# Layer one's attention in stated order on ScalarE and VectorE, without the gates' sum up to the query

## The chip, the cores and the metric

One core of a Trainium2 chip. The metric is the device time of one execution in microseconds; smaller is better. Before the change the median of three runs is 624.39 us (624.07 to 624.49).

## What is computed

Two decoder layers over 256 tokens of width 1024, in float32. Each layer: a norm, one input projection, 12 self-attention heads and 4 heads that attend to 256 memory tokens, an output projection, and a SwiGLU FFN. Layer one's self-attention is the forgetting attention; layer two's has ALiBi slopes instead (with 256 tokens all keys lie in the query's own block).

```
def fox_attention(q, k, v, log_f):
    F = jnp.cumsum(log_f, axis=-1)
...
        s = (jnp.einsum('bhqd,bhkd->bhqk', qb, k).astype(jnp.float32) * scale
             + Fq[..., :, None] - F[..., None, :])
        s = jnp.where(tq[:, None] >= kpos[None, :], s, NEG)
        p = jax.nn.softmax(s, axis=-1)
...
xn = rms_norm(h, norm_mix[i]); mn = rms_norm(mem, norm_mem[i])
...
h = h + heads @ w_out[i]
hn = rms_norm(h, norm_ffn[i])
gu = hn @ w_gate_up[i]
h = h + (jax.nn.silu(gu[..., :D_FF]) * gu[..., D_FF:]) @ w_down[i]
```

`Fq` is the gates' sum up to the query. It is the same number for every key of a query, that is, along a softmax row.

## The kernel before

Every float32 product is made of three matmuls: operands are split into a rounded part (`hi`) and the rest (`lo`), and `prod` (L317) issues hi·hi, lo·hi and hi·lo. Weights stream from HBM in units of up to 1 MB. `split` (L212) halves a unit and splits each half, 128x1024: the rounded part on ScalarE (L224), the rest on VectorE (L227), which needs ScalarE's result. `weights` (L233) calls `split` so that the splits are stated five halves ahead of their use. A unit's buffer is loaded again (L204, on SP's queue) when its last `lo` is made.

`mixer` (L466) is a layer's attention. The value projection comes first. Then three groups `g` of query and key projections (L574 to L601), each for two pairs of heads, 8 steps of 12 matmuls. Before group 1 `memory_heads` (L552) runs: in layer one the memory's key and value projection (`mem_kv`, L340), whose row factors come from two mean squares on ScalarE (`factor`, L257, called at L360) with a power on POOL, then the memory heads' queries (`qm`). After each group the queries and keys are scaled and split (L591 to L601), on ScalarE, VectorE and POOL. Then the output projection (L612), 12 matmuls of 512 columns to a step, and what is left of attention.

Attention itself is a generator for each pair of heads, `attend` (L393). Those alive are advanced by `step()` (L460), once for every two of the 8 projection steps and once for each step of the output projection, so that attention's parts lie between projection matmuls. Its parts, with waiting steps between them: the bias (`bias`, L534) and the score matmuls with bias, maximum, exponentials (L425), reciprocal and products (L429) in one step; two or three steps later the transposes (L436) and their copies out of PSUM (L439 on ScalarE, L440 on VectorE); two steps later the product with the values, and the split of the result into the output projection's operand (L449, by `split_ps`, L245 and L246). In the trace `s_`, `p_`, `pT_` and `o_` are scores, probabilities, their transposes and the outputs; `_m` is memory, `_s` self-attention.

`gate_sums` (L514) makes the sums over the gates: `F_ps` and its copy `fr`, which goes through DRAM to all partitions (`fd`, then `fk`), and `Fq_ps` with its copy `fq`, the sums up to the query. `bias` makes, for a pair of heads in layer one, F minus Fq plus the mask in four VectorE instructions. `wake_exp` (L452) loads the exponential's table early.

PSUM has 8 banks in one pool, `probs` 3 buffers, `work` 7. The whole program runs with TensorE and SP in the order in which it is written (L773). ScalarE, VectorE and POOL are ordered by a planner, by when it believes each instruction ready and by priority, which falls in the order of writing; only layer one's value projection (L479) has ScalarE and VectorE in written order too. Within such a stretch the written order is kept for each engine; where the stretch's instructions fall among those outside it stays the planner's.

Of the kernel before, what the change touches and what calls it, by code (L numbers as in the profile page):

```python
# [27 lines left out]
P = 128  # L29
# [29 lines left out]
TURN_STEPS = 2  # L59

# [78 lines left out]
def trunk(ctx: ExitStack, tc: tile.TileContext, plan, stream, x, gains, norm_final, square, mem, out):  # L139
# [23 lines left out]
    mem_t = [ap.tile([P, 2, 512], F32, tag="probs", name=f"mem{t}", bufs=3).rearrange("p a s -> p (a s)") for t in range(NT)]  # L163
# [176 lines left out]
    def mem_kv(i):  # L340
# [5 lines left out]
        for u in range(2):  # L346
            for kk in range(4):
# [11 lines left out]
                if i == 0 and k == 3:  # L359
                    rs_mem.extend(factor(mem_t[t], f"mem{t}") for t in range(NT))  # L360
# [32 lines left out]
    def attend(name, xq, xk, vt, h0, idle, bias, dst, kt):  # L393
# [16 lines left out]
        pr = ap.tile([P, 2, 512], F32, tag="probs", name=f"p_{name}", bufs=3)  # L410
        for a in range(2):
            for qt in range(NT):
                c = slice(qt * S, qt * S + nk[qt] * P)
                if causal:
                    nc.vector.tensor_tensor_reduce(pr[:, a, c], sb[a].t[:, c], more[qt][:, a], scale=-1.0, scalar=-NEG,  # L415
                                                   op0=ALU.add, op1=ALU.min, accum_out=nmax[:, a, qt:qt + 1])
                else:
                    nc.vector.tensor_reduce(nmax[:, a, qt:qt + 1], sb[a].t[:, c], axis=AX.X, op=ALU.max, negate=True)
        total = sp.tile([P, 2, NT], F32, tag="total", name=f"total_{name}")
        rc = sp.tile([P, 2, NT], F32, tag="rc", name=f"rc_{name}")  # L420
        for a in range(2):
            for qt in range(NT):
                c, j = slice(qt * S, qt * S + nk[qt] * P), slice(qt, qt + 1)
                src, scale = (pr[:, a, c], -1.0) if causal else (sb[a].t[:, c], 1.0)
                nc.scalar.activation(pr[:, a, c], src, AF.Exp, bias=nmax[:, a, j], scale=scale, accum_out=total[:, a, j])  # L425
            nc.vector.reciprocal(rc[:, a], total[:, a])
            for qt in range(NT):
                c = slice(qt * S, qt * S + nk[qt] * P)
                nc.vector.tensor_scalar_mul(pr[:, a, c], pr[:, a, c], rc[:, a, qt:qt + 1])  # L429
        for _ in range(SOFTMAX_STEPS[causal]):  # L430
            yield
# [5 lines left out]
        pT = ap.tile([P, 2, 512], F32, tag="probs", name=f"pT_{name}", bufs=3)  # L437
        width = len(blocks) * P
        nc.scalar.activation(pT[:, 0, :width], tb[0].t[:, :width], AF.Copy)  # L439
        nc.vector.tensor_copy(pT[:, 1, :width], tb[1].t[:, :width])  # L440
# [8 lines left out]
        split_ps(dst[0][:, kt, :], dst[1][:, kt, :], ob.t[:, :S])  # L449
        yield  # L450

    def wake_exp(src):  # L452

        one = sp.tile([P, 1], F32, tag="one", name="one", bufs=1)
        nc.scalar.activation(one, src, AF.Exp, scale=0.0)
# [10 lines left out]
    def mixer(i, xs, rs):  # L466
# [44 lines left out]
        if i == 0:  # L511
            fq = cp.tile([P, NT, H], F32, name="fq")

        def gate_sums():  # L514
# [19 lines left out]
        def bias(h0):  # L534

            b = fk[:, h0:h0 + 2]
            if i == 1:
                return b[:, :, P:], b
            b0 = ap.tile([P, 2, P], F32, tag="bias", name=f"bias{h0}", bufs=1)
            for a in range(2):  # L540
# [33 lines left out]
        for g in range(3):  # L574
            if g == MEM_AT[i]:
                memory_heads()
            kb = [bank(f"qk_ps{i}{2 * g + a}") for a in range(2)]
            for k in range(KD):
                wh, wl = weights(U["qk", i, g][k // 4], k % 4)
                for a in range(2):  # L580
                    for s in range(2):
                        c = slice(a * P, (a + 1) * P)
                        prod(kb[a], kb[a].t[:, s * S:(s + 1) * S], (wh[:, s, c], wl[:, s, c]),
                             (xs[0][:, k, :], xs[1][:, k, :]), k == KD - 1)
                if k % 2:
                    step()
            if g == 0:
                rsb = spread(rs, f"x{i}", (DH ** -0.5, 1.0), "x")
                if i == 0:
                    active.append(gate_sums())  # L590
            for a in range(2):  # L591
                p = 2 * g + a
                qk = ap.tile([P, 2, S], F32, tag="work", name=f"qk{i}{p}", bufs=WORK_BUFS)
                nc.vector.tensor_mul(qk.rearrange("p a s -> p (a s)"), kb[a].t, rsb.rearrange("p a s -> p (a s)"))
                xq = ap.tile([P, 2, S], F32R, tag="work", name=f"xq{i}{p}", bufs=WORK_BUFS)
                xk = ap.tile([P, 2, 2 * S], F32R, tag="pair", name=f"xk{i}{p}", bufs=PAIR_BUFS)
                no_lo(xk)
                split_queries(xq, qk[:, 0])
                split_keys(xk, qk[:, 1])
                idle = a + IDLE[i][g]  # L600
                active.append(attend(f"s{i}{p}", xq, xk, vsb, 2 * p, idle, bias, hT, p))  # L601

        acc = [[bank(f"o_acc{i}{t}{c}") for c in range(2)] for t in range(NT)]

        def o_item(n, j, kk, t, halves=(0, 1)):
            k = 2 * j + kk
            wh, wl = weights(U["out", i][n], kk)
            for c in halves:
                cs = slice(c * 512, (c + 1) * 512)
                prod(acc[t][c], acc[t][c].t, tok(hT, k, t), (wh[:, 0, cs], wl[:, 0, cs]), n == 3 and kk == 1)  # L610

        for n, j in enumerate((3, 0, 1)):  # L612
            for kk in range(2):
                step()
                for t in range(NT):
                    o_item(n, j, kk, t)
        while active:
            step()
# [29 lines left out]
    def ffn(i, xs, late):  # L648
# [5 lines left out]
        def gu(c, kk):  # L654
# [13 lines left out]
            if first:  # L668
                rsb.append(spread(rs, f"f{i}", (1.0,), "f")[:, 0])
# [156 lines left out]
```

## Time and profile before

| | |
|---|---|
| median of three runs | 624.39 us |
| profiled execution | 623.77 us |
| its span, first to last instruction | 622.0 us |
| TensorE, VectorE, ScalarE, POOL busy | 608.5, 455.8, 392.4, 61.6 us |
| layer one's attention and projections | about 11 to 129 us |
| layer one's FFN | 129 to 313 us |
| layer two's attention and projections | 314 to 430 us |
| layer two's FFN and the final norm | 430 to 622 us |

Times in the profile are microseconds from the span's start. A wait is idle time of an engine just before an instruction, with the instruction that ended it. PE is TensorE, DVE is VectorE, ACT is ScalarE, SPq is SP's queue. The profiled execution took 1.77 us more than its span.

### The profile page before, as it was taken

The numbers are of one execution on the slowest core, as the hardware profiler recorded it, in microseconds if no ns is written. First come the engines' busy times: TensorE is split into PE (matmuls) and PEld (weight loads), VectorE is DVE, ScalarE is ACT, GpSimd is POOL, SyncE is SP. The second block draws the span as 40 slices with busy tenths as digits, with TensorE's granted clock in tenths as the row PEclk, the third lists the DMA queues.
The fourth block names the chain that finished last, engine by engine and source line by source line (L and its number), as shares of the span: only waits on it lengthen the run. The fifth ranks groups of instructions, "written<-read, shape, count | busy, mean of one in ns | idle before, by whom it ended". The sixth has DMA issues, their size and how long they took to land.

```text
span 622.0 us, 9564 instructions
## 1 busy us (share of the span) xinstructions
PE 608.5 (98%) x3640; PEld 533.9 (86%) x3640; DVE 455.8 (73%) x827; ACT 392.4 (63%) x737; POOL 61.6 (10%) x90
## 2 busy tenths in 40 slices
PE   8999999999999999999999999999999999999995
PEld 6999887788888888888899999877888888888884
DVE  5677999978677676678675679986867666666664
ACT  7879788575555555557467589865755555555542
POOL 2023122046000000000011032200000000000000
PEclk9999999999999999999999999999999999999999
DMA  8977431525455545555455642332455555555301
GB/s 354 420 276 273 169 136 69 202 96 214 174 195 204 193 173 184 194 203 190 165 187 203 243 144 89 136 135 99 155 191 199 204 188 173 184 199 203 136 1 67
DMA packets 16774, 112.31 MB, mean 181 GB/s; under 512 B 1996, under 2 KB 2008, under 8 KB 4312
## 3 DMA queue, kind: packets, MB, share of 16 engines
q1 hardware_dynamic: 16440, 111.42, 49.1%
q8 instruction: 28, 0.46, 0.3%
q10 hardware_dynamic: 288, 0.29, 0.1%
q14 instruction: 18, 0.15, 0.1%
HBM read 110.64 MB, written 1.06 MB: 180 GB/s over the span
## 4 chain that ended last, share of the span: by engine, by line
PE 81%; DVE 9%; ACT 7%; issue 1%; DMA 1%; SPq 0%; POOLq 0%; POOL 0%; DVEq 0%
PE gu L180 40%; PE d_acc L180 18%; PE qk_ps L180 6%; PE o_acc L180 5%; PE v_ps L180 5%; DVE lo L227 2%; ACT hi L224 2%; DMA raw<-in_stream 1%; PE s_s L180 1%; PE mv_ps L180 1%; PE qm_ps L180 1%; PE mk_ps L180 1%; DVE p_s L415 1%; PE o_s L180 1%; DVE p_s L429 1%
## 5 line engine op out<-in xcount | busy, mean ns | idle before, releaser
L227 DVE TENSOR_TENSOR lo<-raw,hi 128x1024 fp32r<-128x1024 f32 (+3 forms) x201 | 241.0, 1206 | 69.1 <-ACT hi L224 63.8
L224 ACT ACTIVATE hi<-raw 128x1024 fp32r<-128x1024 f32 (+3 forms) x201 | 206.4, 1035 | 73.5 <-PE d_acc L180 47.0
L180 PE MATMUL gu<-x_ffn,hi 128*128 128x512 f32 x704 | 177.5, 392 | 0.0
L180 PEld LDWEIGHTS gu<-x_ffn,hi 128*128 128x128 f32 x704 | 126.3, 189 | 22.2
L180 PE MATMUL d_acc<-hi,h 128*128 128x512 f32 x348 | 107.1, 389 | 0.0
L180 PEld LDWEIGHTS gu<-x_ffn,lo 128*128 128x128 f32 x704 | 96.7, 190 | 8.1 <-ACT x_ffn L248 1.0
L180 PE MATMUL gu<-x_ffn,lo 128*128 128x256 f32 x704 | 100.5, 284 | 0.1
L180 PEld LDWEIGHTS d_acc<-hi,h 128*128 128x128 f32 x348 | 65.3, 188 | 13.6
L180 PE MATMUL qk_ps<-x_x,hi 128*128 128x256 f32 x384 | 72.4, 284 | 0.9 <-ACT p_m L425 0.9
L180 PE MATMUL d_acc<-lo,h 128*128 128x512 f32 x174 | 67.7, 389 | 0.0
L180 PEld LDWEIGHTS qk_ps<-x_x,hi 128*128 128x128 f32 x384 | 60.9, 191 | 1.9 <-ACT p_m L425 1.1
L180 PE MATMUL qk_ps<-x_x,lo 128*128 128x256 f32 x192 | 54.3, 283 | 0.0
L675 ACT ACTIVATE gate<-gu 128x256 f32<-128x256 f32 x44 | 16.9, 384 | 57.6 <-PE gu L180 57.6
L180 PE MATMUL o_acc<-hi,x_hT 128*128 128x512 f32 x128 | 41.7, 405 | 0.5 <-DVE x_hT L246 0.5
L675 ACT ACTIVATE up<-gu 128x256 f32<-128x256 f32 x44 | 16.9, 385 | 39.6 <-PE gu L180 39.4
L180 PEld LDWEIGHTS d_acc<-lo,h 128*128 128x128 f32 x174 | 32.7, 188 | 6.7
L676 DVE TENSOR_TENSOR gate<-gu,gate 128x256 f32<-128x256 f32 x44 | 18.6, 423 | 25.5 <-ACT gate L675 25.5
L180 PEld LDWEIGHTS qk_ps<-x_x,lo 128*128 128x128 f32 x192 | 36.8, 191 | 0.0
L676 DVE TENSOR_TENSOR up<-gu,up 128x256 f32<-128x256 f32 x44 | 18.7, 424 | 24.6 <-ACT up L675 24.6
L180 PE MATMUL v_ps<-hi,x_x 128*128 128x384 f32 (+1 forms) x128 | 33.2, 339 | 0.1
L425 ACT ACTIVATE p_s<-p_s,nmax_s 128x128 f32<-128x128 f32 (+1 forms) x48 | 21.3, 445 | 11.4 <-DVE nmax_s L415 11.4
L180 PEld LDWEIGHTS o_acc<-hi,x_hT 128*128 128x128 f32 x128 | 22.7, 188 | 6.2 <-DVE x_hT L246 1.2
(155 smaller groups left out, 753.7 us busy)
## 6 DMA issues: line engine op xcount, KB each, us to landing
raw<-in_stream SPq DMA_DIRECT2D x94, 1024.0 KB, 4.8
raw<-in_stream SPq DMA_DIRECT2D x3, 1036.0 KB, 7.8
raw<-in_stream SPq DMA_DIRECT2D x4, 768.0 KB, 5.1
fk<-fd SPq DMA_DIRECT2D x3, 512.0 KB, 7.1
raw<-in_stream SPq DMA_DIRECT2D x2, 518.0 KB, 4.2
h<-in_x SPq DMA_DIRECT2D x2, 512.0 KB, 11.9
mem<-in_mem SPq DMA_DIRECT2D x2, 512.0 KB, 12.8
gfin<-in_norm_final SPq DMA_DIRECT2D x1, 512.0 KB, 3.5
```

Source lines behind the costliest of these rows:

```text
L180: nc.tensor.matmul(o, lhsT, rhs, start=self.fresh, stop=stop, skip_group_check=True)
L224: nc.scalar.activation(hi[:, c0:c1], src[:, c0:c1], AF.Copy)
L227: nc.vector.tensor_sub(lo[:, c0:c1], src[:, c0:c1], hi[:, c0:c1].bitcast(F32))
L415: nc.vector.tensor_tensor_reduce(pr[:, a, c], sb[a].t[:, c], more[qt][:, a], scale=-1.0, scalar=-NEG, op0=ALU.add, op1=ALU.min, accum_out= ...
L425: nc.scalar.activation(pr[:, a, c], src, AF.Exp, bias=nmax[:, a, j], scale=scale, accum_out=total[:, a, j])
L429: nc.vector.tensor_scalar_mul(pr[:, a, c], pr[:, a, c], rc[:, a, qt:qt + 1])
L675: nc.scalar.activation(v[:, 1], b[s].t[:, S:], AF.Copy)
L676: nc.vector.tensor_add(v[:, 0], b[s].t[:, :S], v[:, 1])
```

## The change

- ScalarE and VectorE follow the written order in three stretches of layer one: group 1, group 2, and the output projection with what is left of attention. Group 0, the memory projection and the rest stay with the planner.
- In `attend`, for both layers, the softmax, the copies of the transposes and the output's split are marked urgent: the planner takes them as if they stood 75 places earlier.
- `attend` issues the bias one step before the scores, and the reciprocal (one for four rows of sums, not two) and products one step after the exponentials. The number of steps in all is the same.
- `Fq_ps`, six small matmuls, and `fq` are gone. The bias of layer one is F plus the mask: two VectorE adds of 128x256 for a pair of heads.
- The memory's mean squares and powers are stated at the end of group 0.
- `probs` has 4 buffers; the FFN's factors share the attention's `rsb_x` buffer.

```
@@ attend
-        for _ in range(idle):
+        for _ in range(idle - 1):
             yield
         if causal:
             more = bias(h0)
+        yield
         sb = [bank(f"s_{name}_{a}") for a in range(2)]
...
-        pr = ap.tile([P, 2, 512], F32, tag="probs", name=f"p_{name}", bufs=3)
+        pr = ap.tile([P, 2, 512], F32, tag="probs", name=f"p_{name}", bufs=4)
+        with tc.high_priority(offset=URGENT):
             (maxima, with bias where causal; exponentials)
+        yield
+        with tc.high_priority(offset=URGENT):
+            nc.vector.reciprocal(rc.rearrange("p a t -> p (a t)"), total.rearrange("p a t -> p (a t)"))
+            for a in range(2):
+                for qt in range(NT):
+                    c = slice(qt * S, qt * S + nk[qt] * P)
+                    nc.vector.tensor_scalar_mul(pr[:, a, c], pr[:, a, c], rc[:, a, qt:qt + 1])
-        for _ in range(SOFTMAX_STEPS[causal]):
+        for _ in range(SOFTMAX_STEPS[causal] - 1):
             yield
...
+        with tc.high_priority(offset=URGENT):
+            split_ps(dst[0][:, kt, :], dst[1][:, kt, :], ob.t[:, :S])
@@ gate_sums and bias
-            gb = bank("Fq_ps")
-            for t in range(NT):
-                for u in range(t + 1):
-                    gb.mm(gb.t[:, t * H:(t + 1) * H], prefix[:, (t - u) * P:(t - u + 1) * P], lf[:, u], stop=u == t)
-            nc.scalar.activation(fq.rearrange("p t h -> p (t h)"), gb.t[:, :NT * H], AF.Copy)
-            wake_exp(fq[:, 0, 0:1])
+            wake_exp(fr[:, 0:1])
...
-            for a in range(2):
-                for t, o in ((0, b0), (1, b)):
-                    with tc.issue_after(mem_done[i]):
-                        nc.vector.scalar_tensor_tensor(o[:, a], b[:, a, :(t + 1) * P], fq[:, t, h0 + a:h0 + a + 1],
-                                                       mask[:, P - t * P:], op0=ALU.subtract, op1=ALU.add)
+            for t, o in enumerate((b0, b[:, :, P:])):
+                with tc.issue_after(mem_done[i]):
+                    nc.vector.tensor_add(o, b[:, :, t * P:(t + 1) * P], mask[:, P:].unsqueeze(1).to_broadcast([P, 2, P]))
@@ mem_kv and mixer
-                if i == 0 and k == 3:
-                    rs_mem.extend(factor(mem_t[t], f"mem{t}") for t in range(NT))
...
+            with tc.manual_schedule(engines={ACT, DVE}) if g >= MEM_AT[i] and i == 0 else nullcontext():
                 (group g: projection, steps, query and key splits)
+                if i == g == 0:
+                    rs_mem.extend(factor(mem_t[t], f"mem{t}") for t in range(NT))
...
+        with tc.manual_schedule(engines={ACT, DVE}) if i == 0 else nullcontext():
             (output projection and the remaining steps)
@@ ffn
-                rsb.append(spread(rs, f"f{i}", (1.0,), "f")[:, 0])
+                rsb.append(spread(rs, f"f{i}", (1.0,), "x")[:, 0])
```

Lines in parentheses stand for code that is moved in by one level and not otherwise changed.

## Rows read from the trace of the kernel before

**Rows 1.** The page's busy times (us, share of the span, instructions; here TensorE's) and, of the 40 equal slices of the span, the busy tenths of TensorE and VectorE and the granted TensorE clock.
```profile
PE 608.5 (98%) x3640; PEld 533.9 (86%) x3640; DVE 455.8 (73%) x827; ACT 392.4 (63%) x737; POOL 61.6 (10%) x90
...
PE   8999999999999999999999999999999999999995
...
DVE  5677999978677676678675679986867666666664
...
PEclk9999999999999999999999999999999999999999
```
**Rows 2.** Windows: for each stretch its length, then busy us (and instructions) of PE, PEld, DVE, ACT and POOL, the granted clock, the DMA share and GB/s. Two stretches of layer one's attention, then the like part of layer two.
```profile
62.20:94.60 32.40, 31.06 (x255) 28.25 (x253) 32.15 (x97) 25.26 (x68) 6.59 (x11) 1.00 0.40 146
94.60:121.50 26.90, 25.57 (x146) 20.01 (x144) 26.05 (x76) 19.64 (x50) 3.23 (x4) 1.00 0.32 115
355.00:430.00 75.00, 74.20 (x531) 65.17 (x530) 61.40 (x163) 55.86 (x142) 13.99 (x20) 1.00 0.37 127
```
**Rows 3.** TensorE's waits, us in total, times, longest: first from 20 to 135 us (layer one), then from 355 to 432 us (layer two).
```profile
PE s_s L180 <- DVE pT_s L440: 1.0, 1, 1.0
PE rsb_ps_mem L180 <- POOL rs_mem L269: 0.9, 2, 0.7
PE qk_ps L180 <- ACT p_m L425: 0.9, 1, 0.9
...
PE s_s L180 <- DVE nmax_s L415: 0.3, 1, 0.3
...
PE o_m L180 <- ACT pT_m L439: 0.6, 1, 0.6
PE o_acc L180 <- DVE x_hT L246: 0.2, 1, 0.2
```
**Rows 4.** TensorE's timeline in layer one: start, us, line, operation, shapes, count, idle time before and its releaser.
```profile
42.28 0.84 PE L180 MATMUL Fq_ps<-lf,sq 128*128 128x12 f32 x6
42.98 0.37 PE L180 MATMUL mk_ps<-x_mem,hi 128*128 128x256 f32 x1
...
49.67 0.49 PE L180 MATMUL rsb_ps_mem<-sq,rs_mem 128*128 128x128 f32 x2 [0.69 <-POOL rs_mem L269]
...
50.60 0.36 PE L180 MATMUL qm_ps<-x_x,hi 128*128 128x256 f32 x1
...
62.21 1.21 PE L180 MATMUL s_m<-mk,xqm 128*128 128x256 f32 x8
...
72.62 0.36 PE L180 MATMUL qk_ps<-x_x,hi 128*128 128x256 f32 x1
...
77.33 1.18 PE L436 MATMUL pT_m<-sq,p_m 128*128 128x128 f32 x8 [0.46 <-DVE nmax_s L415]
78.27 0.36 PE L180 MATMUL qk_ps<-x_x,hi 128*128 128x256 f32 x1
...
81.22 0.82 PE L436 MATMUL pT_s<-sq,p_s 128*128 128x128 f32 x6
...
121.52 0.73 PE L180 MATMUL o_acc<-hi,x_hT 128*128 128x512 f32 x2
...
123.01 0.50 PE L180 MATMUL o_acc<-hi,x_hT 128*128 128x512 f32 x1 [0.30 <-DVE x_hT L246]
```
**Rows 5.** ScalarE's timeline in layer one: the first scaling after group 0, the first of the memory's two mean squares, the first of a pair's four exponentials, and the weight half after them.
```profile
35.89 0.66 ACT L280 ACTIVATE rsb_x<-rsb_ps_x 128x256 f32<-128x256 f32 x2 [3.22 <-PE rsb_ps_x L180]
...
47.32 1.04 ACT L254 ACTIVATE junk_mem<-mem 128x1024 bf16<-128x1024 f32 x1
...
66.42 0.47 ACT L425 ACTIVATE p_m<-s_m,nmax_m 128x256 f32<-128x256 f32 x1 [1.50 <-DVE nmax_m L418]
...
68.23 1.07 ACT L224 ACTIVATE hi<-raw 128x1024 fp32r<-128x1024 f32 x1
```
**Rows 6.** VectorE's timeline: the memory queries' splits, a memory pair's maxima, then a self-attention pair's bias, first score instruction, the weight split after the four, and a pair's four products, all in layer one; last, a weight split of layer two.
```profile
61.59 1.73 DVE L382 TENSOR_TENSOR xqm<-qm,xqm 64x256 fp32r<-64x256 f32 x2
...
65.63 1.41 DVE L418 TENSOR_REDUCE nmax_m<-s_m 128x1 f32<-128x256 f32 x4
...
106.33 0.61 DVE L543 SCALAR_TENSOR_TENSOR bias<-fk,fq,sq 128x128 f32<-128x128 f32 x2
106.86 0.88 DVE L543 SCALAR_TENSOR_TENSOR fk<-fk,fq,sq 128x256 f32<-128x256 f32 x2
107.66 0.28 DVE L415 CUSTOM_DVE_ANT_0 p_s<-s_s,bias 128x128 f32<-128x128 f32 x1
...
108.77 1.22 DVE L227 TENSOR_TENSOR lo<-raw,hi 128x1024 fp32r<-128x1024 f32 x1
...
110.29 1.00 DVE L429 TENSOR_SCALAR p_s<-p_s,rc_s 128x128 f32<-128x128 f32 x4
...
421.98 1.22 DVE L227 TENSOR_TENSOR lo<-raw,hi 128x1024 fp32r<-128x1024 f32 x1
```
**Rows 7.** The page's DMA issues: KB each, and us from issue to landing.
```profile
fk<-fd SPq DMA_DIRECT2D x3, 512.0 KB, 7.1
...
mem<-in_mem SPq DMA_DIRECT2D x2, 512.0 KB, 12.8
```
**Rows 8.** SP's timeline: when the memory rows' and the gate sums' loads were issued.
```profile
17.89 0.90 SPq L196 DMA_DIRECT2D mem<-in_mem  x2
...
52.77 2.36 SPq L532 DMA_DIRECT2D fk<-fd  x3
```

More of the change, by code (lines that the diff above doesn't have):

```diff
@@ L59 @@
 TURN_STEPS = 2
+URGENT = 75
 def _slopes():
@@ L160, in trunk @@
     nc.gpsimd.memset(minus_half, -0.5)
-    mem_t = [ap.tile([P, 2, 512], F32, tag="probs", name=f"mem{t}", bufs=3).rearrange("p a s -> p (a s)") for t in range(NT)]
+    mem_t = [ap.tile([P, 2, 512], F32, tag="probs", name=f"mem{t}", bufs=4).rearrange("p a s -> p (a s)") for t in range(NT)]
     def load_x():
@@ L419, in attend @@
[L419 to L429, printed above, removed]
@@ L430, in attend @@
-        for _ in range(SOFTMAX_STEPS[causal]):
+        pr = ap.tile([P, 2, 512], F32, tag="probs", name=f"p_{name}", bufs=4)
[3 more added lines that the diff above has]
+                    c = slice(qt * S, qt * S + nk[qt] * P)
+                    if causal:
+                        nc.vector.tensor_tensor_reduce(pr[:, a, c], sb[a].t[:, c], more[qt][:, a], scale=-1.0, scalar=-NEG,
+                                                       op0=ALU.add, op1=ALU.min, accum_out=nmax[:, a, qt:qt + 1])
+                    else:
+                        nc.vector.tensor_reduce(nmax[:, a, qt:qt + 1], sb[a].t[:, c], axis=AX.X, op=ALU.max, negate=True)
+            total = sp.tile([P, 2, NT], F32, tag="total", name=f"total_{name}")
+            rc = sp.tile([P, 2, NT], F32, tag="rc", name=f"rc_{name}")
+            for a in range(2):
+                for qt in range(NT):
+                    c, j = slice(qt * S, qt * S + nk[qt] * P), slice(qt, qt + 1)
+                    src, scale = (pr[:, a, c], -1.0) if causal else (sb[a].t[:, c], 1.0)
+                    nc.scalar.activation(pr[:, a, c], src, AF.Exp, bias=nmax[:, a, j], scale=scale, accum_out=total[:, a, j])
@@ L448, in attend @@
             ob.mm(o[:, 2 * S - width:S], vt[1][:, h0 + a, :], pT[:, a, S:width], stop=True)
-        split_ps(dst[0][:, kt, :], dst[1][:, kt, :], ob.t[:, :S])
+        with tc.high_priority(offset=URGENT):
+            split_ps(dst[0][:, kt, :], dst[1][:, kt, :], ob.t[:, :S])
         yield
     def wake_exp(src):
-        one = sp.tile([P, 1], F32, tag="one", name="one", bufs=1)
+        one = sp.tile([P, 1], F32, tag="one", name="one", bufs=1)[:src.shape[0]]
         nc.scalar.activation(one, src, AF.Exp, scale=0.0)
@@ L587, in mixer @@
[L587 to L613, printed above, removed]
+            with tc.manual_schedule(engines={ACT, DVE}) if g >= MEM_AT[i] and i == 0 else nullcontext():
+                kb = [bank(f"qk_ps{i}{2 * g + a}") for a in range(2)]
+                for k in range(KD):
+                    wh, wl = weights(U["qk", i, g][k // 4], k % 4)
+                    for a in range(2):
+                        for s in range(2):
+                            c = slice(a * P, (a + 1) * P)
+                            prod(kb[a], kb[a].t[:, s * S:(s + 1) * S], (wh[:, s, c], wl[:, s, c]),
+                                 (xs[0][:, k, :], xs[1][:, k, :]), k == KD - 1)
+                    if k % 2:
+                        step()
+                if i == g == 0:
+                    rs_mem.extend(factor(mem_t[t], f"mem{t}") for t in range(NT))
+                if g == 0:
+                    rsb = spread(rs, f"x{i}", (DH ** -0.5, 1.0), "x")
+                    if i == 0:
+                        active.append(gate_sums())
+                for a in range(2):
+                    p = 2 * g + a
+                    qk = ap.tile([P, 2, S], F32, tag="work", name=f"qk{i}{p}", bufs=WORK_BUFS)
+                    nc.vector.tensor_mul(qk.rearrange("p a s -> p (a s)"), kb[a].t, rsb.rearrange("p a s -> p (a s)"))
+                    xq = ap.tile([P, 2, S], F32R, tag="work", name=f"xq{i}{p}", bufs=WORK_BUFS)
+                    xk = ap.tile([P, 2, 2 * S], F32R, tag="pair", name=f"xk{i}{p}", bufs=PAIR_BUFS)
+                    no_lo(xk)
+                    split_queries(xq, qk[:, 0])
+                    split_keys(xk, qk[:, 1])
+                    idle = a + IDLE[i][g]
+                    active.append(attend(f"s{i}{p}", xq, xk, vsb, 2 * p, idle, bias, hT, p))
@@ new lines, in mixer, with o_item @@
+        with tc.manual_schedule(engines={ACT, DVE}) if i == 0 else nullcontext():
+            acc = [[bank(f"o_acc{i}{t}{c}") for c in range(2)] for t in range(NT)]
+            def o_item(n, j, kk, t, halves=(0, 1)):
+                k = 2 * j + kk
+                wh, wl = weights(U["out", i][n], kk)
+                for c in halves:
+                    cs = slice(c * 512, (c + 1) * 512)
+                    prod(acc[t][c], acc[t][c].t, tok(hT, k, t), (wh[:, 0, cs], wl[:, 0, cs]), n == 3 and kk == 1)
+            for n, j in enumerate((3, 0, 1)):
+                for kk in range(2):
+                    step()
+                    for t in range(NT):
+                        o_item(n, j, kk, t)
+            while active:
```

31 lines of the change are left out of this document (6 added, 25 removed).

## The prediction

> **What bounds the kernel now.** I read the page first, then the windows, then TensorE's waits, then the timelines around them. [...] VectorE's slices are full, or nearly so, in slices 5 to 8, layer one's attention, and nowhere else for as long [rows 1]. The windows say it sharper: VectorE is busy 32.15 of 32.4 us from 62.2 and 26.05 of 26.9 from 94.6, while TensorE loses 1.34 and 1.33 us there; layer two's like stretch loses 0.8 of 75 [rows 2]. So in this stage VectorE, with ScalarE behind it, sets the pace, and TensorE's waits name these two (and POOL once) [rows 3].
>
> The rows understate the loss, as matmul ends are modelled. 24 projection matmuls take 2.95 us from 78.27 to 81.22; from 72.62 the same 24 take 4.71, to 77.33: 1.8 went, where 0.88 is shown there and the 0.46 after it [rows 4]. At that ratio the 1.0 and 0.3 us before two score blocks [rows 3] are some 1.9. At the tail, four wide matmuls (about 0.9) take 121.52 to 123.01: 0.6 [rows 4]. The memory factors cost 1.25 (below). Sum for layer one some 5.6 us.
>
> **Part 1: the memory's factors earlier, no gate sum up to the query.** The two mean squares now run on ScalarE at 47.32 us, two of 1.04 [rows 5], and TensorE waits 0.9 us for what POOL makes of them [rows 3]. They need only the memory rows, issued at 17.89 [rows 8] and landed 12.8 us later [rows 7], near 31; ScalarE stands idle for 3.22 us just before 35.89 [rows 5]. There the 2.1 us fit at no cost; if they don't, they stay ahead of the attention as now, at no loss. They issue no DMA; on POOL the two powers go ahead of query splits that start later; SP's order is untouched. The six Fq matmuls go: 42.98 - 42.28 = 0.70 us of TensorE [rows 4], and their 0.2 us copy; the table load hangs on another tile and stays. From about 48.95 (end of the memory projections, 24 matmuls a 2.95 us block back from 49.67 less the 0.7 wait) to 50.60 is 1.65 us for 0.4 of broadcast [rows 4]: 1.25 goes. Sum -1.95, and ScalarE, busy without a gap from 35.89 until the first exponentials, comes 2.1 us earlier to them: both arrive together, so the gain holds up to there.
>
> **Part 2: the bias.** Before, four instructions for a pair of heads, 106.33 to 107.66: 1.33 us [rows 6]. After, two plain adds of 128x256. No row shows them. Nearest are the fused form, 0.88 for two of that size, and a weight split of 1024 elements, 1.22, a quarter of which is 0.3: 0.6 to 0.9 a pair [rows 6]. I take 0.75, between its own slope and the fused form. That frees 0.6 us for each of six pairs, 3.5 us of VectorE, none of TensorE by itself. [...] The bias also goes one step ahead of the scores; the gate sums it reads are issued from 52.77 [rows 8] and land in 7.1 us [rows 7], about 60, and it is wanted near 62.
>
> **Part 3: the stated order.** It holds within three stretches (second projection group, third, output projection); across their borders the planner still merges. I walk the first border, where slack is least. TensorE reaches the first memory scores at 62.21 - 1.95 = 60.3 us [rows 4]. VectorE ends its query splits at 63.3 - 2.1 = 61.2, and one weight split more at 62.35 [rows 6]. Then in stated order: bias 0.75, four maxima 1.4 (64.5). The next weight split on VectorE needs ScalarE's half, and that now stands behind four exponentials (66.42 to 68.23, 1.81) [rows 5]; the last ends 0.8 us after the last maximum, the half takes 0.95, so VectorE stands still for 1.8 us, to 66.3. Split 1.13, scores with bias 1.11, bias 0.75, reciprocal and products 1.1, maxima 1.4 (71.8) [rows 6]. Again 1.8 us behind exponentials, of which a split of the next stretch can fill 1.1. Split (74.8), products 1.1, scores 1.11, copy 0.55, half the last products 0.6: 78.2. TensorE, which could transpose at 74.9, does so at 78.2, where it did at 77.33 before [rows 4]. The lead of 1.95 becomes 0.85 behind: **+2.8 us**. Behind each waiting split stand the next pair's scores, and TensorE waits for what follows from them.
>
> Then VectorE has copy 0.55, output split 0.4, bias and weight split, 2.9 us, for a step of 2.95 and 1.7 us on TensorE, and catches up; the next transposes come two steps after their products, so 78 to 94 us is costed at -0.2. In the output projection its steps are of 2.6 to 4 us against 3.5 to 4.6 on TensorE: copies and maxima that made TensorE wait at 103 and 108 come straight after their cause, and 1.9 us goes. The cover is thin: with another VectorE microsecond a step, half returns. The fourth probability buffer lets a transposed block leave PSUM without waiting for a slot; it is within these sums. Its room comes in part from a tile shared with the FFN's factors, last read long before it is written again: nothing. At the tail, copy and output split now precede the weight split: -0.6.
>
> Layer one: -1.95 + 2.8 - 0.2 - 1.9 - 0.6 = -1.85 us.
>
> **Part 4: layer two, urgency alone.** The planner stays; attention comes up to 75 places sooner. Two waits are shown, 0.6 and 0.2 us [rows 3]; ahead of the second, a weight split of 1.22 us runs before the output splits (421.98) [rows 6]. Weight splits that are put off have a lead of five halves to hide in, about 14 us at 2.95 each. Bounds: -1.1 (both waits and what the modelled ends hide) to +0.5 (one like those of layer one opens); I take -0.5, the tail's alone.
>
> **Sum**: -2.4 us. The profiled execution took 623.77 us, 1.77 outside its span, 0.6 below the median of 624.39; 621.4 on its scale is 622.0 on the median's. A measurement can tell about 0.2%, 1.25 us, from no change.
>
> **Rivals.**
> (a) *Lockstep decides.* The 1.8 us stalls recur in each step that ends in maxima or scores, and at the second border too the products queue behind exponentials. With 1.2 more at the first border (no filler from the next stretch), 2.0 at the second, and the waits of 103 and 108 kept: -1.95 + 4.0 + 2.0 - 0.6 - 0.5 = +3, 627.3. The sign turns where the borders cost over 3 us with those waits kept, over 5 with them gone. For it: VectorE has 0.25 us to spare in 32 [rows 2]. Against it: 3.5 us of its work goes. [...]
> (b) *VectorE's relief is enough.* Every wait of layer one goes, and the gate matmuls: -5.6 - 0.7, with layer two's -0.5 it is -6.8: 617.6. For it: VectorE was the only full engine. Against it: the 1.8 us stalls, which no freed work removes.
> (c) *Nothing left.* The lead is lost at the border, and the output stage's waits move to bank releases: -1.95 + 2.8 - 0.6 - 0.5, 624.1. The change not doing what it says (the planner's order being the stated one already) falls here, less part 1.
>
> **How the numbers follow.** Forecast 0.45 (620.2 to 623.1), (b) 0.20, (c) 0.17, (a) 0.18. Faster by over 0.2%, below 623.1: 0.65. Within: 0.17. Slower: 0.18. The range reaches to both outer rivals' own times, 617.6 to 627.3; what lies beyond them is their outer halves, about 0.19.
>
> **What would show it.** Right: squares before 36 us, no wait for the memory's factors; VectorE gaps of 1 to 2 us ahead of weight splits near 64 and 72, released by ScalarE; the second memory transposes near 78; no score waits after 100; FFN one starting 1.9 us sooner. Wrong: a TensorE wait over 5 us between 74 and 80, or one at the second border; no wait at all near 78, which is (b); or the stretch from FFN one's start to the end getting longer, which puts the loss in layer two.

## The result: 0.85% slower, and the profile after

The changed kernel takes 629.42 us (median; 629.21 to 629.99) against 624.23 for the kernel before in the same series: ratio 1.0085, 95% interval 1.0067 to 1.0102. The forecast was 622.0 with a range up to 627.3; the time lies above that range, 2.1 us beyond rival (a). The profiled execution took 629.21 us with a span of 627.4, 5.4 more than before's 622.0. Every line number of the attention is a few higher now: L180 is L183, L224 and L227 are L227 and L230, L418 is L421, L425 is L428, L429 is L435, L436 is L442.

The page after: busy times of TensorE and VectorE, then TensorE, VectorE and the granted clock in 40 slices; they answer to [rows 1].
```profile
PE 611.3 (97%) x3634; PEld 536.8 (86%) x3634; DVE 451.6 (72%) x799; ACT 393.1 (63%) x736; POOL 63.3 (10%) x90
...
PE   9999889999999999999999999999999999999995
...
DVE  5677788888766766668775579886876666676664
...
PEclk9999889999999999999999999999999999999999
```
VectorE lost 4.2 us of work, and its four full slices have become a 7 and three 8s. TensorE has two 8s where it had 9s, and in the same two slices its granted clock is down too. The windows of the first two stretches of [rows 2] say the same:
```profile
62.20:94.60 32.40, 27.75 (x199) 25.47 (x198) 26.00 (x72) 20.05 (x55) 5.30 (x8) 0.89 0.31 109
94.60:121.50 26.90, 26.19 (x160) 20.93 (x159) 21.63 (x69) 20.02 (x56) 4.63 (x6) 1.00 0.31 113
```
In the first stretch VectorE is busy 26.00 us, was 32.15, and ScalarE 20.05, was 25.26: no engine is full there any more, and TensorE loses 4.65 us instead of 1.34. A part of that is only that a window of the same length holds less of the program now (TensorE has 199 matmuls in it, was 255). Still, the engine that was the bound has less to do, and the stretch is longer. Such a picture suggests that the engines wait for each other. TensorE's waits from 20 to 145 us, which answer to the first part of [rows 3]:
```profile
PE pT_m L442 <- DVE p_m L435: 3.5, 2, 2.8
PE qk_ps L183 <- ACT p_m L428: 1.2, 1, 1.2
PE s_m L183 <- POOL xqm L383: 0.8, 1, 0.8
PE o_acc L183 <- DVE x_hT L249: 0.8, 2, 0.6
PE s_s L183 <- DVE pT_s L447: 0.7, 1, 0.7
```
TensorE's timeline, to be held against [rows 4]:
```profile
48.53 0.36 PE L183 MATMUL qm_ps<-x_x,hi 128*128 128x256 f32 x1
...
61.13 1.09 PE L183 MATMUL s_m<-mk,xqm 128*128 128x256 f32 x7 [0.84 <-POOL xqm L383]
...
71.61 1.37 PE L442 MATMUL pT_m<-sq,p_m 128*128 128x128 f32 x8 [0.66 <-DVE p_m L435]
74.15 0.39 PE L183 MATMUL qk_ps<-x_x,hi 128*128 128x256 f32 x1 [1.17 <-ACT p_m L428]
...
81.67 1.94 PE L442 MATMUL pT_m<-sq,p_m 128*128 128x128 f32 x8 [2.82 <-DVE p_m L435]
...
86.98 0.82 PE L442 MATMUL pT_s<-sq,p_s 128*128 128x128 f32 x6
...
122.06 0.50 PE L183 MATMUL o_acc<-hi,x_hT 128*128 128x512 f32 x1 [0.58 <-DVE x_hT L249]
```
The memory query projection begins 2.07 us sooner (48.53, was 50.60). The second memory transposes begin 4.34 later (81.67, was 77.33), the self-attention's transposes behind them 5.76 later (86.98, was 81.22). FFN one starts at 134.49, was 129.00 (5.49 later), and FFN two's first matmul comes 5.14 later. So the whole loss is made between 49 and 87 us, where a lead of 2.07 us turns into a lag of 5.76: 7.8 us.

VectorE in that stretch (start, us, operation, and in brackets its idle time before and the releaser):
```profile
63.42 0.42 DVE L543 TENSOR_TENSOR bias<-fk,sq 128x256 f32<-128x256 f32 x1
63.75 0.42 DVE L543 TENSOR_TENSOR fk<-fk,sq 128x256 f32<-128x256 f32 x1
64.09 1.41 DVE L421 TENSOR_REDUCE nmax_m<-s_m 128x1 f32<-128x256 f32 x4
67.79 1.23 DVE L230 TENSOR_TENSOR lo<-raw,hi 128x1024 fp32r<-128x1024 f32 x1 [2.29 <-ACT hi L227]
...
72.30 1.40 DVE L421 TENSOR_REDUCE nmax_m<-s_m 128x1 f32<-128x256 f32 x4
75.99 1.23 DVE L230 TENSOR_TENSOR lo<-raw,hi 128x1024 fp32r<-128x1024 f32 x1 [2.28 <-ACT hi L227]
...
77.22 1.20 DVE L230 TENSOR_TENSOR lo<-raw,hi 128x1024 fp32r<-128x1024 f32 x1
...
81.17 1.14 DVE L435 TENSOR_SCALAR p_m<-p_m,rc_m 128x256 f32<-128x256 f32 x4
```
and ScalarE beside it:
```profile
64.87 0.47 ACT L428 ACTIVATE p_m<-s_m,nmax_m 128x256 f32<-128x256 f32 x1 [3.67 <-DVE nmax_m L421]
...
66.68 1.07 ACT L227 ACTIVATE hi<-raw 128x1024 fp32r<-128x1024 f32 x1
...
73.08 0.47 ACT L428 ACTIVATE p_m<-s_m,nmax_m 128x256 f32<-128x256 f32 x1 [1.95 <-DVE nmax_m L421]
...
74.89 2.01 ACT L227 ACTIVATE hi<-raw 128x1024 fp32r<-128x1024 f32 x2
```
Read the two together. ScalarE stands idle for 3.67 us until the first maxima come, though the rounded half of the next weight split needs only weights; that half runs at 66.68, behind the four exponentials. VectorE has finished its maxima at 65.50, and its next instruction is the remainder of that very split: it stands for 2.29 us. The same comes again at 73 to 76. Each engine waits in turn for the other.

### The profile page after: what moved, and what is told of

The parts are those of the page before. It is cut to its first block, busy times and chain, and to the rows that moved or that the text cites. A ratio compares the mean times of both kernels' runs of the same rounds, so it can differ in the third digit from the quotient of the medians.

```text
span 627.4 us, 9521 instructions
## 1 busy us (share of the span) xinstructions
PE 611.3 (97%) x3634; PEld 536.8 (86%) x3634; DVE 451.6 (72%) x799; ACT 393.1 (63%) x736; POOL 63.3 (10%) x90
## 4 chain that ended last, share of the span: by engine, by line
PE 82%; DVE 7%; ACT 7%; issue 3%; POOL 0%; POOLq 0%; ACTq 0%; DVEq 0%
PE gu L183 39%; PE d_acc L183 18%; PE qk_ps L183 7%; PE v_ps L183 5%; PE o_acc L183 4%; DVE lo L230 3%; ACT hi L227 2%; PE s_s L183 1%; PE mv_ps L183 1%; PE mk_ps L183 1%; ACT p_s L428 1%; PE warm_ps L183 1%; PE pT_s L442 1%; DVE p_s L435 1%; PE o_s L183 1%
## 5 line engine op out<-in xcount | busy, mean ns | idle before, releaser
L230 DVE TENSOR_TENSOR lo<-raw,hi 128x1024 fp32r<-128x1024 f32 (+3 forms) x201 | 240.2, 1201 | 76.0 <-ACT hi L227 70.9
L227 ACT ACTIVATE hi<-raw 128x1024 fp32r<-128x1024 f32 (+3 forms) x201 | 206.4, 1036 | 68.4 <-PE d_acc L183 47.0
L183 PE MATMUL gu<-x_ffn,hi 128*128 128x512 f32 x704 | 177.5, 392 | 0.0
L183 PEld LDWEIGHTS gu<-x_ffn,hi 128*128 128x128 f32 x704 | 126.3, 189 | 22.2
L183 PE MATMUL d_acc<-hi,h 128*128 128x512 f32 x348 | 107.1, 389 | 0.0
L183 PEld LDWEIGHTS gu<-x_ffn,lo 128*128 128x128 f32 x704 | 96.7, 190 | 8.1 <-ACT x_ffn L251 1.0
L183 PE MATMUL gu<-x_ffn,lo 128*128 128x256 f32 x704 | 100.5, 284 | 0.1
L183 PEld LDWEIGHTS d_acc<-hi,h 128*128 128x128 f32 x348 | 65.3, 188 | 13.6
L183 PE MATMUL qk_ps<-x_x,hi 128*128 128x256 f32 x384 | 74.4, 290 | 1.2 <-ACT p_m L428 1.2
L183 PE MATMUL d_acc<-lo,h 128*128 128x512 f32 x174 | 67.7, 389 | 0.0
L183 PEld LDWEIGHTS qk_ps<-x_x,hi 128*128 128x128 f32 x384 | 62.8, 197 | 2.2 <-ACT p_m L428 1.4
L183 PE MATMUL qk_ps<-x_x,lo 128*128 128x256 f32 x192 | 55.3, 288 | 0.0
L183 PE MATMUL o_acc<-hi,x_hT 128*128 128x512 f32 x128 | 41.9, 405 | 0.9 <-DVE x_hT L249 0.9
L183 PEld LDWEIGHTS d_acc<-lo,h 128*128 128x128 f32 x174 | 32.7, 188 | 6.8
L183 PEld LDWEIGHTS qk_ps<-x_x,lo 128*128 128x128 f32 x192 | 37.9, 197 | 0.0
L183 PE MATMUL v_ps<-hi,x_x 128*128 128x384 f32 (+1 forms) x128 | 33.2, 341 | 0.0
L428 ACT ACTIVATE p_s<-p_s,nmax_s 128x128 f32<-128x128 f32 (+1 forms) x48 | 21.3, 445 | 12.1 <-DVE nmax_s L418 12.0
L183 PEld LDWEIGHTS o_acc<-hi,x_hT 128*128 128x128 f32 x128 | 22.9, 188 | 6.8 <-DVE x_hT L249 1.9
```

The costliest lines, as they stand in the source:

```text
L183: nc.tensor.matmul(o, lhsT, rhs, start=self.fresh, stop=stop, skip_group_check=True)
L227: nc.scalar.activation(hi[:, c0:c1], src[:, c0:c1], AF.Copy)
L230: nc.vector.tensor_sub(lo[:, c0:c1], src[:, c0:c1], hi[:, c0:c1].bitcast(F32))
```

## The experiments

**Theories.** (T1) The loss is made by the written order of the first stretch (second projection group): weight halves behind exponentials on ScalarE hold up VectorE. (T2) It is made by the two later stretches or by the urgency in both layers. (T3) The early factors and the plain bias themselves make something late.

### Where the loss lies

**no_order**: the changed kernel with the written order taken out of all three stretches.
```
-            with tc.manual_schedule(engines={ACT, DVE}) if g >= MEM_AT[i] and i == 0 else nullcontext():
+            with nullcontext():
...
-        with tc.manual_schedule(engines={ACT, DVE}) if i == 0 else nullcontext():
+        with nullcontext():
```


> The changed kernel with its three stretches of written order given back to the planner; all else of the change kept. Theory one (the written order costs the 5.2 us: in the first stretch a weight split on VectorE stands behind four exponentials on ScalarE): 620 to 623 us, no VectorE wait of over 2 us for a weight half between 60 and 80, TensorE's clock full there. Rival (the loss comes from the urgency and the planner's new merging, or from the other edits): 627 to 630.

Measured: 622.23 us, ratio 0.9967 (0.9954 to 0.9980). That is 7.2 us less than the changed kernel, with the urgency kept: T3 is out, and so is the urgency by itself, one half of T2.

**order_first** and **order_rest**: the written order in the first stretch alone, and in the other two alone (`g == 1` or `g == 2` in place of `g >= MEM_AT[i]`; in the first, the output projection's order is out as well).

> The changed kernel with written order in the first stretch alone (second projection group); second and third stretch to the planner. Theory one: the loss stays, 628 to 631 us, the memory transposes near 81. Rival (second border and output projection carry it): 621 to 624.

> The changed kernel with written order in the second and third stretch, the first to the planner. Theory one: 620.5 to 623.5 us, memory transposes near 76. Rival (second border): 626 to 629.

Measured: 628.31 us, 1.0066 (1.0051 to 1.0081), and 622.61 us, 0.9977 (0.9967 to 0.9986). The first stretch alone carries the loss. The two later ones neither give nor cost anything that these intervals can tell from no_order, so the rest of T2 is out, and no gain of the order shows there.

**order_alone**: the kernel before with only the three written orders.

> The kernel before, with nothing but the three stretches of written order. Theory one: slower by what the first border cost, some 6 to 9 us, 630 to 633. Rival (written order costs only together with the moved reciprocal, bias and urgency): 623 to 626.

Measured: 635.33 us, 1.0173 (1.0157 to 1.0190), above what was expected. Put alone into the kernel before, the order costs 11.3 us; taken out of the changed kernel, it gives back 7.2. The profiled execution (636.73 us) shows that the two losses are not of one kind:
```profile
81.91 1.94 PE L436 MATMUL pT_m<-sq,p_m 128*128 128x128 f32 x8 [3.02 <-DVE nmax_s L415]
```
The second memory transposes come as late as in the changed kernel (81.67), and the self-attention's behind them at 88.27, 7.05 us later than before. But from 61 to 85 us VectorE never waits for a half, and its longest wait is 0.43 us, for exponentials: here the products stand in one step with them, ahead of the next split, and VectorE is busy for 8.88 of the 10 us from 70 to 80. From 88 us to FFN one (141.94, was 129.00) another 5.9 us go, in stretches where the order cost the changed kernel nothing. So the rest of the change hides a part of the order's price; which part of it does (plain bias, moved products, urgency, fourth buffer), no run shows.

### What in the first stretch

**split_first**: the changed kernel with each weight split asked for one step sooner, so that in stated order it stands ahead of that step's softmax.
```
                     if k % 2:
+                        if i == 0 and g >= 1 and k + 1 < KD:
+                            weights(U["qk", i, g][(k + 1) // 4], (k + 1) % 4)
+                        elif i == 0 and g == 1:
+                            weights(U["qk", i, 2][0], 0)
                         step()
...
                 for kk in range(2):
+                    if i == 0:
+                        weights(U["out", i][n], kk)
                     step()
```


> The changed kernel with written order kept, but in layer one's three stretches each weight split is stated ahead of the attention step that it stood behind (the weights of the next projection step are asked for before the step is taken). Theory one (the loss is the split on VectorE waiting for a half behind exponentials): the two VectorE waits of 2.3 us near 66 and 74 go, TensorE keeps its full clock, 621.5 to 624.5 us. Rival (any written order loses here, since scores and maxima then stand behind splits): 627 to 630.

Measured: 630.02 us, 1.0091 (1.0079 to 1.0103): a miss. VectorE's splits in it:
```profile
62.82 2.36 DVE L230 TENSOR_TENSOR lo<-raw,hi 128x1024 fp32r<-128x1024 f32 x2
65.77 1.41 DVE L421 TENSOR_REDUCE nmax_m<-s_m 128x1 f32<-128x256 f32 x4
69.46 1.23 DVE L230 TENSOR_TENSOR lo<-raw,hi 128x1024 fp32r<-128x1024 f32 x1 [2.29 <-ACT hi L227]
...
77.34 1.23 DVE L230 TENSOR_TENSOR lo<-raw,hi 128x1024 fp32r<-128x1024 f32 x1 [2.29 <-ACT hi L227]
```
The edit moved all splits by one step together: one more came before the maxima, which are later by 1.7 us, and behind the maxima stood the split after it, with its half behind the same exponentials. The two gaps are 2.29 us as they were. It left the pattern as it was, and so it was no test of T1.

**scalar_free**: a proper test. In the first stretch the written order holds VectorE alone.
```
-            with tc.manual_schedule(engines={ACT, DVE}) if g >= MEM_AT[i] and i == 0 else nullcontext():
+            with tc.manual_schedule(engines={DVE} if g == 1 else {ACT, DVE}) if g >= MEM_AT[i] and i == 0 else nullcontext():
```


> The changed kernel; in the first stretch (second projection group) the written order holds VectorE alone, and ScalarE's is the planner's again. VectorE's order is instruction for instruction that of the changed kernel; on ScalarE the rounded halves of the weight splits now come ahead of the exponentials. If what costs the time is VectorE standing still for halves that wait behind exponentials, the two gaps of 2.3 us go, the second memory transposes come at 76 to 78 instead of 81.7, and the time is 622.5 to 625. If VectorE has simply too much to do at this place, or the order of its own work is at fault (scores behind splits, the filler split), the gaps move elsewhere and it stays at 628 to 630.

Measured: 622.56 us, ratio 0.9984 (0.9975 to 0.9992). In 5 of its 11 executions it took 623.2 to 623.8, which is why the ratio, a mean, stands nearer to 1 than the median; three of those five have a mean granted clock of 0.993 to 0.995, where the six others have 0.996 to 0.999, but what they did in that stretch is not recorded. ScalarE, then VectorE, from 60 to 77 us:
```profile
61.33 2.01 ACT L227 ACTIVATE hi<-raw 128x1024 fp32r<-128x1024 f32 x2
64.98 0.47 ACT L428 ACTIVATE p_m<-s_m,nmax_m 128x256 f32<-128x256 f32 x1 [1.64 <-DVE nmax_m L421]
```
```profile
64.20 1.41 DVE L421 TENSOR_REDUCE nmax_m<-s_m 128x1 f32<-128x256 f32 x4
65.53 1.21 DVE L230 TENSOR_TENSOR lo<-raw,hi 128x1024 fp32r<-128x1024 f32 x1
...
71.03 1.21 DVE L230 TENSOR_TENSOR lo<-raw,hi 128x1024 fp32r<-128x1024 f32 x1
...
76.19 1.14 DVE L435 TENSOR_SCALAR p_m<-p_m,rc_m 128x256 f32<-128x256 f32 x4
```
Two halves now fill ScalarE's idle time before the maxima. VectorE does the same work in the same order, and both of its gaps are gone: the split starts at 65.53 instead of 67.79, the last products at 76.19 instead of 81.17. The second memory transposes begin at 76.69, 4.98 us sooner, and FFN one at 128.14, 6.35 sooner. On ScalarE one more thing has moved: a copy of the first memory transposes comes at 72.29, ahead of four exponentials, instead of 81.34 behind them; no instruction of VectorE waited for it. This is T1, shown: the place of a few halves on ScalarE, which was not the full engine, is worth 6.9 us between the medians, 6.3 by the two ratios, with what the clock adds (below) included.

**vector_free**: the other way round, `{ACT}` in place of `{DVE}`.

> The changed kernel; in the first stretch the written order holds ScalarE alone, and VectorE's is the planner's. The halves still stand behind exponentials on ScalarE, but on VectorE products and scores may pass the waiting remainder. If the loss is made by the two queues together (a half behind exponentials, and VectorE's work behind that remainder), freeing either one ends most of it: 622.5 to 626. If ScalarE's order alone is what costs, TensorE waits for the weights themselves, or for the late exponentials, and it stays over 627.

Measured: 622.93 us, 0.9983 (0.9974 to 0.9992). Either queue alone may keep the stated order; both together may not. In this one the first half still comes behind the exponentials (67.12 to 68.19), but the planner has put the products, the scores and the next maxima ahead of its remainder on VectorE, which waits 1.34 us where it waited 2.29:
```profile
67.28 0.18 DVE L431 RECIPROCAL rc_m<-total_m 128x4 f32<-128x4 f32 x1 [1.34 <-ACT p_m L428]
...
71.07 1.19 DVE L230 TENSOR_TENSOR lo<-raw,hi 128x1024 fp32r<-128x1024 f32 x1
```

### What TensorE's clock adds

Windows of the changed kernel over the place, with the granted clock third from the end:
```profile
74.00:78.00 4.00, 3.85 (x19) 3.81 (x20) 2.01 (x3) 2.90 (x8) 0.00 (x0) 0.60 0.00 0
...
82.00:86.00 4.00, 4.00 (x24) 4.00 (x24) 3.57 (x11) 2.86 (x7) 1.72 (x2) 0.62 0.13 53
```
Cut finer, it is 0.50 from about 75 to 78 and from about 82 to 85, and 1.00 before, between and after. TensorE had stood still for 0.66 and 1.17 us ahead of the first fall, for 2.82 ahead of the second. The first lies within the wait for the products and costs nothing by itself; the second stretches the block from the second transposes (81.67) to the next ones (86.98), 5.31 us, where before needed 3.89 (77.33 to 81.22).

**fill** and **fill_second**: the changed kernel with matmuls on a zero operand, which add nothing, in TensorE's waits; in the first, 5 in the first wait and 18 in the second, in the other 10 in the second alone.
```
+        if name == "m01":
+            fill(last_kb[0][0], FILL)
         tb = [bank(f"pT_{name}_{a}") for a in range(2)]
```


> The changed kernel with 5 and 18 more matmuls of 512 columns that add zero, put where TensorE stands still before and after the first memory transposes and before the second (about 4 us of work inside waits). Theory one, with the clock as a second part: VectorE's chain is as it was, the transposes at 81.7 as before, but TensorE stays at full clock and the 1.4 us that transposes and projection after them lose at half clock come back: 627.6 to 628.4. Rival (the clock costs nothing, since the slow stretch lies inside waits): 629.2 to 629.8.

Measured: 636.52 us, 1.0195 (1.0182 to 1.0208): a miss, by the experiment's own fault. Its first five matmuls wrote to the bank whose scores VectorE was still to read, and waited 6.96 us for it:
```profile
79.95 2.50 PE L184 MATMUL s_s<-zero,mk 128*128 128x512 f32 x5 [6.96 <-DVE nmax_s L428]
```
TensorE stood still longer, not shorter, and nothing follows for the clock.

> The changed kernel with 10 matmuls of 512 columns on a zero operand (they add nothing) ahead of the second memory transposes, into the accumulation that TensorE holds anyway: some 2.1 us of TensorE in a wait of 2.8. If TensorE's clock falls because it stands still there, the granted clock is higher from 81 to 85 and the time 1 to 1.4 us shorter, 628.0 to 628.5. If the fall comes of the wait before (73 to 74), or TensorE's clock there costs nothing because VectorE sets the pace, the time stays at 629.1 to 629.9.

Measured: 627.92 us, 1.0069 (1.0056 to 1.0081), 1.5 us less than the changed kernel, with matmuls added. The windows of it:
```profile
74.00:78.00 4.00, 3.63 (x27) 3.43 (x28) 1.79 (x3) 3.12 (x8) 0.00 (x0) 1.00 0.00 0
...
82.00:86.00 4.00, 4.00 (x34) 3.87 (x34) 3.27 (x11) 2.85 (x8) 1.47 (x2) 1.00 0.21 88
```
The second transposes begin no sooner (81.88), but the block behind them takes 3.96 us (81.88 to 85.84) instead of 5.31. So between these two traces the clock's fall costs 1.35 us, on top of the wait. The whole kernels say it less sharply: 1.5 us between the medians, 1.0 by the two ratios, and the two intervals overlap. Four of the five executions, with a mean granted clock of 0.997, took 627.8 to 628.2 us; the fifth, at 0.993, took 629.98, like the changed kernel's own four (629.2 to 630.0 us at 0.992 to 0.995). So the added matmuls go with a higher clock in most executions and not in all. The first fall is absent in the trace as well, ahead of the added matmuls, after waits of 0.42 and 1.17 us; why it came in one and not in the other stays open, and with it whether it was the added matmuls that kept the second away.

### What the other parts are worth

**early_factors**: the kernel before with the memory's two factors asked for before its first query scaling, and nothing else.

> The kernel before with only the memory's factors stated at the end of group 0. Prediction's part 1 without the gate matmuls: memory queries 1.2 us sooner; by the prediction that holds, 622.5 to 623.3. Rival (ScalarE's freed 2.1 us is taken up at the first border): within 0.3 us of before.

Measured: 624.22 us, 1.0004 (0.9995 to 1.0012): no gain. The median stands between two groups, six executions of 623.5 to 623.7 us and six of 624.7 to 625.5. The profiled one (624.94) is of the second; two of TensorE's waits in its layer one, and then a line of its timeline:
```profile
PE qk_ps L180 <- ACT p_m L423: 2.0, 2, 1.1
PE s_s L180 <- ACT pT_s L437: 2.0, 1, 2.0
```
```profile
103.02 1.98 PE L180 MATMUL s_s<-xk,xq 128*128 128x256 f32 x8 [1.95 <-ACT pT_s L437]
```
The memory's own wait of 0.9 us is gone [rows 3], and these waits have grown from 0.9 and 1.0. TensorE is 1.32 us ahead of before at the first memory scores (60.89), 0.62 at 100.25, and loses this lead, and more, at the wait ahead of 103.02: behind it TensorE runs slower from about 104 to 107 (a pair of output matmuls of 512 columns takes 1.05 us at 104.79 and at 106.07, and 0.62 from 107.30 on), and FFN one begins at 130.20, 1.20 us later than before. What the six quicker executions did there is not recorded.

**parts12**: this, no gate sum up to the query, and the plain bias; no order, no urgency.
```
-            for a in range(2):
-                for t, o in ((0, b0), (1, b)):
...
+            for t, o in enumerate((b0, b[:, :, P:])):
+                with tc.issue_after(mem_done[i]):
+                    nc.vector.tensor_add(o, b[:, :, t * P:(t + 1) * P], mask[:, P:].unsqueeze(1).to_broadcast([P, 2, P]))
```


> The kernel before with the memory's factors stated early, the gate sums up to the query left out and the plain bias of two adds; no written order, no urgency, three probability buffers. By the prediction's parts 1 and 2: 2 us sooner at the memory queries, and VectorE 0.6 us a pair freer: 620.5 to 622.5. Rival (the lead is lost at the border between the projection groups, where buffers and VectorE hold): 623.5 to 624.5.

Measured: 621.90 us, 0.9964 (0.9952 to 0.9975), FFN one at 127.37. This is the lowest median of the study. no_order, which has the moved steps, the urgency and the fourth buffer besides, can't be told from it (0.9967), so those three show no gain.

**pool_bias**: parts12 with the two additions on GpSimd (`nc.gpsimd.tensor_add`).

> The kernel before with the memory's factors earlier, no gate sum up to the query, and the plain bias, without any written order and without the urgency; and the two bias additions of a pair are on GpSimd instead of VectorE. If VectorE's load is still what bounds layer one's attention, some 3.5 to 4 us less of it shortens the time by 0.5 to 2 us against the same kernel with the additions on VectorE (621.9): 620 to 621.4. If ScalarE's or the halves' queue bounds it by now, it stays at 621.5 to 622.3; if GpSimd's own queue makes the memory queries or the split queries late, it is 622.5 to 624.

Measured: 622.27 us, 0.9973 (0.9962 to 0.9984): the same as parts12. VectorE's groups by line from 62 to 94 us (busy us and mean ns of one), of parts12 and then of pool_bias:
```profile
L227 DVE TENSOR_TENSOR lo<-raw,hi 128x1024 fp32r<-128x1024 f32 x9 | 10.9, 1217 | 0.1
...
L427 DVE TENSOR_SCALAR p_m<-p_m,rc_m 128x256 f32<-128x256 f32 x8 | 3.0, 414 | 0.0
```
```profile
L227 DVE TENSOR_TENSOR lo<-raw,hi 128x1024 fp32r<-128x1024 f32 x9 | 11.7, 1323 | 0.1
L427 DVE TENSOR_SCALAR p_m<-p_m,rc_m 128x256 f32<-128x256 f32 x8 | 3.9, 537 | 0.0
```
The additions cost GpSimd 10.4 us there (ten of them, 0.75 us on average for one buffer and 1.26 for the other). VectorE's slow splits lie within GpSimd's main run of them (61.9 to 70.1 us): two of the three splits there took 1.65 and 1.76 us, the third 1.21; the six after it took 1.21 to 1.22. Of the 3.7 us that left VectorE, these two groups alone give 1.7 back, and its busy time in the stretch falls from 31.78 us only to 31.36. So VectorE was hardly relieved, and whether its load still bounds parts12 stays open.

## Why the prediction was wrong, by its steps

**Part 1 held up to the memory's queries, and no further.** The squares run at 32.62 and 33.66 us, the wait for the memory's factors is gone, and the lead is 2.07 us at the query projection (forecast 1.95). But the forecast had it last to the first exponentials, and it does not: at the first memory scores it is 1.08 (61.13, was 62.21), since three weight halves now run on ScalarE ahead of the queries' halves, and TensorE waits 0.84 us for POOL's query splits, a wait that the forecast didn't have. In early_factors, which is this step alone, nothing is left of it at the end.

**Part 2 held.** The two additions take 0.67 us a pair (63.42 to 64.09; forecast 0.75). The duration shown is 0.42 each, but the second starts 0.33 us after the first, and it is the starts that count. Parts 1 and 2 together give 2.1 us without the order.

**The step that failed is part 3, "the first border: +2.8".** The mechanism was there as put, VectorE standing still twice behind exponentials; its size was not. The forecast had the second transposes at 78.2, 0.85 us later than before; they came at 81.67, 4.34 later. That is 3.5 us more, or +6.3 for +2.8. Step by step along VectorE: its bias begins at 63.42 and not at 62.35 (1.1, the late query splits); the first gap is 2.29 and not 1.8 (0.5); the products take 1.47 and not 1.1 (0.4); the second gap is 2.28 (0.5); and the filler split, costed inside the second gap, came behind it at 77.22 (1.1). It could not have run inside: its own half is the second of the two at 74.89 on ScalarE, behind the same exponentials, and ended at 76.90, after the gap. Sum 3.6; the first 1.1 of it is Part 1's lost lead. The reciprocal behind the second split shows what a waiting split does to the rest of the queue: ScalarE had ended its sums at 71.13 us, and it ran at 77.13, after the gap.

**The clock was not foreseen at all**: "78 to 94 us ... -0.2" measured +1.4, all of it in the one block whose granted clock fell to 0.50. The trace of before had the granted clock at 1.00 in both stretches of this stage [rows 2], and a wait of TensorE was priced by its length alone.

**The output stage's -1.9 and the tail's -0.6 did not come**: from the first output matmuls (5.71 us later than before) to FFN one (5.49) only 0.2 was won. (At the forecast's own ratio, 1.8 us gone for 1.34 shown, the two waits it counted there come to 1.75 and not 1.9.) The waits near 103 and 108 shrank, and at 116.7 TensorE was down to 4.89 us behind; then it waited 0.58 us at 122.06 for an output split, which stood behind one more weight split held up for its half, again one behind four exponentials on ScalarE (the half began at 119.36):
```profile
120.44 1.23 DVE L230 TENSOR_TENSOR lo<-raw,hi 128x1024 fp32r<-128x1024 f32 x1 [1.99 <-ACT hi L227]
121.59 0.42 DVE L249 TENSOR_TENSOR x_hT<-o_s,x_hT 128x256 fp32r<-128x256 f32 x1
...
126.25 1.22 DVE L230 TENSOR_TENSOR lo<-raw,hi 128x1024 fp32r<-128x1024 f32 x1
127.38 0.76 DVE L249 TENSOR_TENSOR x_hT<-o_s,x_hT 128x256 fp32r<-128x256 f32 x2
```
The last two lines are the tail: a split still precedes the output splits, against the forecast. Why the planner put it there stays open.

**Part 4** measured -0.35 us (FFN one to FFN two's first matmul, 301.23 to 300.88) for -0.5.

Together: 3.5 + 1.6 + 2.3 + 0.15, some 7.5 us between a forecast of -2.4 and a result of +5.2. **The rivals.** (a) was the side that came true, by its mechanism at the first border and once more in the output stage, not at the second border. Held against it was that 3.5 us of VectorE's work goes; but ScalarE sets the length of the gap, from the end of the maxima (65.50) through four exponentials and the half to 67.79, and work taken from VectorE shortens none of that, as the prediction itself says under (b). The time still lies 2.1 us beyond (a), which had no term for the clock. (b)'s relief shows in parts12, worth 2.1 us, far from 6.8. The sign the prediction named for "wrong", a wait over 5 us from 74 to 80, did not appear in the changed kernel (the longest there is 2.82 us, up to 81.67); order_first shows one, 5.17 us, up to 82.85.

## What to carry to other kernels

Where two engines hand pieces to each other in both directions (maxima one way, halves the other), a written order on both must be walked on both queues at once: for each instruction that waits, ask whether its producer's queue has something in front that waits for this engine, and if so move the producer into that queue's idle time or leave one of the two queues free. Price a gap at a queue's head with no filler, unless the filler's own input is there before the gap ends, and price a wait of TensorE like those here (1.17 and 2.82 us in the changed kernel) with the possibility of a lower clock behind it (0.50 for about 3 us, 1.35 us in the second block). VectorE's relief came with a gain in parts12 (2.1 us), where VectorE hardly waits for a half (0.1 us from 62 to 94), and with none in the changed kernel, where it waits for 4.9 us there.

## What the runs showed of the hardware

In the changed kernel TensorE's granted clock fell from 1.00 to 0.50 twice, for about 3 us each time, after idle times of 0.66 and 1.17 us, and of 2.82 us. In order_first it was 0.50 from 82 to 86 after 5.17 us, and the matmuls' pace stayed down to about 88.6 (a pair of 128x256 took 0.63 us up to 88.22, and 0.40 at 88.81). In early_factors the pace was down for about 3 us after 1.95 us of idle time (1.05 us for a pair of 128x512, then 0.62). The clock stayed at 1.00 after 1.99 us at the place of the second fall (fill_second), and after 2.78 us at 75.56 in order_alone. So in these traces the length of the idle time alone does not tell whether it falls. The block from the second memory transposes to the next ones took 3.96 us without a fall, 5.31 with the one of 3 us, and 6.43 in order_first.

In the changed kernel two plain adds of 128x256 fp32 on VectorE start 0.33 us apart (63.42 and 63.75) and show 0.42 each, and the maxima behind them start at 64.09; the durations overlap, so a sum of them counts some 0.08 us too much for each.

Work moved from VectorE to GpSimd came back in part as slower VectorE: with the additions on GpSimd a weight split took 1323 ns on average (1.65 and 1.76 us for two that lay beside the additions), without 1217, and a product of 128x256 took 537, without 414 (pool_bias against parts12).
